# Attention stage of a hybrid trunk: small VectorE operations move to ScalarE, GpSimd and DMAs, and the scan reads its ones from PSUM

## The chip, the cores and the metric

The kernel runs on one core of a Trainium2 chip. The metric is the device time of one execution in microseconds (us). A core has a tensor engine for matmuls (TensorE, PE in the profile; PEld is its loading of weights), a vector engine (VectorE, DVE), a scalar engine (ScalarE, ACT), a general engine (GpSimd, POOL), and a queue engine that issues transfers here (SyncE, SP). Each engine takes its instructions in the order in which they stand in its own queue, and waits on semaphores for the others.

## What is computed

One layer on 1024 tokens of width 1024, all float32: a projection gives queries, keys and values for 8 heads of 64 and a convolution branch; both branches go through one output projection that is added to x, and a gated feed-forward block follows. The change lies in the attention:

```
z    = (q_t . k_s) / sqrt(64)                     # q, k normalised per head
beta = sigmoid(z);   log_one_minus = log_sigmoid(-z), masked to s < t
tail = reverse cumulative sum of log_one_minus over s, without the element itself
o_t  = sum over s < t of  beta[t,s] * exp(tail[t,s]) * v_s
x    = x + concat([attention, conv]) @ w_out
```

The kernel computes exp(tail) as a running product: the sigmoid of -z is taken, and a scan multiplies along the row from its end to its start.

## The kernel before

The stages follow one another: projections and convolution (about the first 257 us), attention with the convolution's half of the output projection between its groups (to about 508 us), the attention's half of the output projection with the second norm, the up projection, and the down projection.

Attention goes head by head (h = 0 to 7), and in a head through four groups g of 256 queries; a group is two blocks u of 128 queries, so that block tb = 2g + u has w = (tb + 1) * 128 keys to look at: scans of 128, 256 ... 1024 columns in a head. Work on a group is spread over three steps: `scores` of group i + 2, `weights` of group i + 1 and `values` of group i are written interleaved, by the positions in `at_value`, `at_score` and `at_weight`; `prep(i + 3)` prepares keys, queries and values of what comes. What stands in an engine's queue is then set by a scheduler that goes over the written program with a timing model of its own, so that a change in one place can move rows in others.

- `scores` (L471): PE makes z in a PSUM tile from the high and low parts of q (L490, L493, mask L492); ACT writes sigmoid(-z) into one of four row buffers `nb` (L494) and sigmoid(z) into `wt` (L495).
- `weights` (L499): DVE scans `nb` in place, multiplying by a column of ones `one` that is read w times (L505); then `wt` is multiplied by `nb` (L506), on DVE where w is 1024 and on GpSimd in the seven other blocks.
- `values` (L508): PE turns `wt` into a PSUM bank `wT` (L527), the rounded copy `th` is made (L533: on DVE in group 0, on ACT in groups 1 to 3), DVE makes the rest `tl` = wT - th (L537), PE adds the products with v to `po` (L543, L544). `finish` moves `po` to `attn_out` (ACT L554, DVE L555).
- `prep_k`, `prep_v`, `prep_q`: GpSimd splits keys and values (L418, L419) and writes each query twice side by side (L445); PE turns them (L430, L449); the turned keys go from PSUM to SBUF in two halves, one on DVE and one on ACT (both L433); ACT and DVE split the queries (L451, L452).
- `out_proj_conv(t)`, one token tile per head, is the list `between`: SP loads x (L400), PE multiplies (L158 to L160), DVE adds the product to x (L404, two halves), SP stores the sum (L406). The split of the activations `m` is L154 on ACT and L155 on DVE.

PSUM has eight banks: three in pool "s" (for `kT`, `qT`, `wT`), two in "o" (for `po` and the projection), two in "z", and one, `psx`, lent to a pool by `bank`: with `shared = "s"` every fourth bank of kind "s" comes from it, so that "s" has four in attention. After attention, `load_wo` fetches the other four row blocks of w_out (`rawo`) and splits them into `hio` (L154) and `loo` (L155), `out_proj_attn(t)` multiplies, adds x2 on DVE (L714) and stores; in the queues before, parts of this stand between rows of head 7.

Of the kernel before, what the change touches and what calls it, by code (L numbers as in the profile page):

```python
# [8 lines left out]
F32 = mybir.dt.float32  # L9
# [7 lines left out]
P = 128  # L17
S = 1024
# [20 lines left out]
def kernel(  # L39
# [32 lines left out]
    def f32(ap):  # L72
        return ap.bitcast(F32)
# [25 lines left out]
    def const(shape, dt, name):  # L99
        return cst.tile(shape, dt, tag=name, name=name)  # L100
# [244 lines left out]
        for _ in project(part, blk):  # L345
            pass
    in_ctx.close()
    shared = "s"
    turns["s"] = 0
    psz_ctx.close()  # L350
    psz = psz_ctx.enter_context(tc.tile_pool(name="ps_z", bufs=2, space=PSUM, reuse_waits="tile"))

    one = const([P, 1], F32, "one")
    nc.vector.memset(one, 1.0)


# [38 lines left out]
    def out_proj_conv(t):  # L395
        tile_of = {}

        def load():
            tile_of["x"] = ap_.tile([P, D], F32, tag="xt", name=f"xt{t}", bufs=2)
            nc.sync.dma_start(tile_of["x"], x_t[t])  # L400

        def add(n, cols, ps):
            xt = tile_of["x"]
            nc.vector.tensor_tensor(xt[:, cols], ps, xt[:, cols], op=ALU.add)  # L404
            if n == 1:
                nc.sync.dma_start(x_part[t], xt)  # L406

        first, *rest = out_proj(ap_, 1, t, conv_out, w_conv, add)
        return [lambda: (load(), first())] + rest
# [12 lines left out]
    def prep_k(h):  # L422

        blk, c0 = h // 4, (h % 4) * DH
        kst = part_of(keys, 1 + h % 2, S)
        khl = token_split(qkv["k", blk][:, :, c0:c0 + DH], part_of(keys, 0, S))
        for half in range(2):
            pt = bank("s", [P, 512], f"kT{h}_{half}", F32R)
            for i in range(4):
                nc.tensor.transpose(pt[:, i * P:(i + 1) * P],  # L430
                                    khl[:, 4 * half + i, :, :].rearrange("p a d -> p (a d)"), ident_r)
            copy = nc.scalar.copy if half else nc.vector.tensor_copy
            copy(kst[:, half * 512:(half + 1) * 512], f32(pt))  # L433
        return kst

    def prep_v(h):
        blk, c0 = h // 4, (h % 4) * DH
        return token_split(qkv["v", blk][:, :, c0:c0 + DH], part_of(rest, h % 2, S), e=h % 2)

    def prep_q(h, half):  # L440
        blk, c0 = h // 4, (h % 4) * DH
        spare = attn_out[:, 3, :] if h < 4 else qkv["q", 0].rearrange("p t c -> p (t c)")
        qd = part_of(spare, half, 512).rearrange("p (t a d) -> p t a d", a=2, d=DH)
        src = qkv["q", blk][:, 4 * half:4 * half + 4, c0:c0 + DH]
        nc.gpsimd.tensor_scalar(qd, src.unsqueeze(2).to_broadcast([P, 4, 2, DH]), 1.0, 0.0,  # L445
                                op0=ALU.mult, op1=ALU.add)
# [52 lines left out]
    def weights(i, u):  # L499
        w = (2 * (i % NG) + u + 1) * P  # L500
        o = S - w
        wt, nb = wts[i, u], nbq[i, u]
        rev = nb[:, S - 1:o - 1:-1] if o else nb[:, S - 1::-1]
        eng = nc.vector if w == S else nc.gpsimd
        return [lambda: nc.vector.tensor_tensor_scan(rev, rev, one.to_broadcast([P, w]), 1.0, op0=ALU.mult, op1=ALU.bypass),  # L505
                lambda: eng.tensor_tensor(wt[:, :w], wt[:, :w], nb[:, o + 1:S + 1], op=ALU.mult)]  # L506

    def values(i, sp):  # L508

# [19 lines left out]
        def high():  # L529
            nonlocal n_th  # L530
            n_th += 1
            d["th"] = part_of(rest, 6 + n_th % 2, 512).rearrange("p (j t) -> p j t", j=2)
            (nc.scalar.copy if g else nc.vector.tensor_copy)(d["th"], d["pt"])  # L533

        def low():
            d["tl"] = ap_.tile([P, 2, 256], F32R, tag="tl", name=f"tl{h}_{g}_{sp}")
# [26 lines left out]
    at_value = {"t": (0.07, 1.05, 4, 5.53), "h": (1.42, 3, 4.7, 7), "l": (2.87, 3.2, 5.2, 7.1), "p": (3.3, 6.33, 7.2, 7.3)}  # L563
    at_score = ((3.43, 2.27), (4.32, 2.05))
    at_weight = ((-0.19, 3.76), (3.43, 6.55))
    prep(0)
    for i in range(n_nb):
        nbs.append(ap_.tile([P, S + 1], F32, tag=f"nb{i}", name=f"nb{i}", bufs=1))
        nc.vector.memset(nbs[i][:, S:S + 1], 1.0)
    for i in range(-2, n_groups):  # L570
# [13 lines left out]
            finish(i)  # L584
        if i + 3 < n_groups:
            prep(i + 3)
        while between and n_between - len(between) < (i + 3) * n_between // (n_groups + 2) + FILL:
            between.pop(0)()
    at_ctx.close()
# [340 lines left out]
```

## Time and profile before

| | |
|---|---|
| Runs shown | median 1206.94 us of 3 (1205.44 to 1211.38) |
| The profiled execution | 1207.02 us, of which the profile's span is 1205.2 us; 16496 instructions |
| Busy in the span | PE 95%, PEld 80%, DVE 80%, ACT 53%, POOL 50% |
| TensorE clock granted, mean | 0.98 |
| DMA | 103.95 MB, mean 86 GB/s |

A row of instructions in the profile names the line, the engine and the operation, what is written from what (buffer numbers left out), the shape and the count; then the time that it kept the engine busy and the mean of one in ns; then how long the engine was idle just before, and what ended that. A row by stretches gives the busy time of PE, PEld, DVE, ACT and POOL in each stretch with their counts, then the granted clock, the DMA share and GB/s. A row by source line gives shortest, median and longest duration in ns. In a row of the timeline the first number is the start, the second the duration, and `x2` two instructions told together.

### The profile page before, as it was taken

To read this page: it belongs to the slowest core of one execution; us is meant where nothing else is said; L and a number is where in the kernel's file an instruction comes from. 1 tells how busy PE (TensorE), PEld (TensorE's weight loads), DVE (VectorE), ACT (ScalarE), POOL (GpSimd) and SP (SyncE) were. 2 spreads that over 40 slices of the span, in tenths; PEclk is the share of its full clock that TensorE was granted. 3 is DMA by queue.
4 is the path that set the end of the run, shared out by engine and by line. 5 is a ranking of instruction groups with operands and counts; after the bars stand their busy time and mean duration, and the time that the engine had idled before them with its cause. 6 is when DMAs were issued, how large, how long until landed. Compare 5 with 4: busy or idle time off the path is not lost.

```text
span 1205.2 us, 16496 instructions
## 1 busy us (share of the span) xinstructions
PE 1141.8 (95%) x5926; PEld 958.6 (80%) x5926; DVE 958.9 (80%) x1167; ACT 633.8 (53%) x1371; POOL 608.6 (50%) x466
## 2 busy tenths in 40 slices
PE   7999999988888888997999999999999999999998
PEld 5888999977777777775888888888888877888887
DVE  6399998468988889789887777777777579978887
ACT  6346667655665567366444333333434356666762
POOL 4068973455755554168643322332233157778873
PEclk9999999998998899998999999999999999999999
DMA  7121111011011013353232222323222261333133
GB/s 246 39 70 53 35 36 36 19 56 68 36 36 36 36 35 107 126 188 105 71 105 70 88 88 71 97 65 101 70 88 83 92 230 67 140 140 114 41 126 140
DMA packets 82080, 103.95 MB, mean 86 GB/s; under 512 B 3438, under 2 KB 63054, under 8 KB 81998
## 3 DMA queue, kind: packets, MB, share of 16 engines
q1 hardware_dynamic: 81710, 101.84, 25.1%
q8 instruction: 47, 0.77, 0.3%
q10 hardware_dynamic: 288, 1.05, 0.2%
q14 instruction: 35, 0.29, 0.1%
HBM read 78.76 MB, written 24.12 MB: 85 GB/s over the span
## 4 chain that ended last, share of the span: by engine, by line
PE 74%; DVE 12%; POOL 5%; issue 4%; ACT 3%; DMA 1%; SPq 0%; POOLq 0%; DVEq 0%; ACTq 0%
PE dn L890 16%; PE u_S L160 6%; PE u_S L159 6%; PE u_S L158 6%; PE u L160 5%; PE u L159 5%; PE u L158 5%; DVE nb L505 4%; DVE tl L537 2%; PE po L544 1%; PE wT L527 1%; POOL conv_out L283 1%; DVE conv L277 1%; PE op L160 1%; PE op L158 1%
## 5 line engine op out<-in xcount | busy, mean ns | idle before, releaser
L890 PE MATMUL dn<-wd,wd 128*128 128x512 f32 x924 | 213.8, 392 | 5.1 <-DVE c L893 2.6
L890 PEld LDWEIGHTS dn<-wd,wd 128*128 128x128 f32 x924 | 172.6, 188 | 46.0 <-DVE c L893 4.6
L893 DVE TENSOR_TENSOR c<-dn,c 128x512 f32<-128x512 f32 x144 | 95.2, 683 | 25.2 <-PE dn L890 23.9
L506 POOL TENSOR_TENSOR wt<-wt,nb 128x128 f32<-128x128 f32 (+6 forms) x56 | 80.2, 1444 | 68.3 <-DVE nb L505 56.2
L277 DVE SCALAR_TENSOR_TENSOR conv<-cpad,cols_b,conv 128x1024 f32<-128x1024 f32 x84 | 108.2, 1288 | 2.4
L283 POOL TENSOR_TENSOR conv_out<-conv_out,attn_out 128x1024 f32<-128x1024 f32 x32 | 81.3, 2540 | 53.0 <-ACT attn_out L282 51.0
L801 ACT CAST wd<-rawd 128x512 fp32r<-128x512 f32 x154 | 85.4, 618 | 39.8 <-DMA rawd<-act_d 24.0
L505 DVE TENSOR_TENSOR_SCAN nb<-nb,one 128x128 f32<-128x128 f32 (+3 forms) x64 | 97.3, 1544 | 4.7 <-ACT nb L494 4.6
L154 ACT CAST aS<-rawu 128x512 fp32r<-128x512 f32 x66 | 40.7, 620 | 99.8 <-PE u_S L160 58.9
L699 POOL TENSOR_TENSOR s<-rawu 128x512 f32<-128x512 f32 x21 | 30.2, 1440 | 124.1 <-DMA rawu<-in_w_up_dram 123.5
L800 ACT COPY whole<-rawd 128x512 f32<-128x512 f32 x110 | 63.4, 585 | 40.3 <-DVE wd L802 18.8
L802 DVE TENSOR_TENSOR wd<-whole,wd 128x512 fp32r<-128x512 f32 x110 | 73.5, 683 | 8.3 <-ACT whole L800 7.2
L802 POOL TENSOR_TENSOR wd<-rawd,wd 128x512 fp32r<-128x512 f32 x44 | 57.4, 1327 | 35.5 <-ACT wd L801 34.8
L154 ACT CAST a<-rawu 128x512 fp32r<-128x512 f32 x66 | 40.8, 621 | 56.6 <-PE u_S L160 37.7
L544 PE MATMUL po<-tl,rest 128*128 128x256 f32 x160 | 50.7, 336 | 19.1 <-DVE tl L537 19.0
L527 PE MATMUL wT<-ident,wt 128*128 128x128 f32 x288 | 50.8, 295 | 17.4 <-POOL wt L506 15.7
L494 ACT ACTIVATE nb<-z 128x512 f32<-128x512 f32 (+3 forms) x96 | 48.0, 501 | 35.6 <-PE z L493 31.6
L757 DVE SCALAR_TENSOR_TENSOR y<-gv,cols_a,y 128x1023 f32<-128x1023 f32 (+1 forms) x44 | 57.8, 1314 | 10.3 <-ACT y L755 10.3
L155 DVE TENSOR_TENSOR aS<-rawu,aS 128x512 fp32r<-128x512 f32 x66 | 63.1, 959 | 3.2 <-ACT aS L154 2.8
L155 DVE TENSOR_TENSOR a<-rawu,a 128x512 fp32r<-128x512 f32 x65 | 48.9, 753 | 16.4 <-ACT a L154 16.4
L705 POOL TENSOR_TENSOR rawu<-rawu 128x512 f32<-128x512 f32 x22 | 31.0, 1411 | 58.1 <-DVE a L155 56.2
L533 ACT CAST rest<-wT 128x512 fp32r<-128x512 f32 x72 | 41.7, 596 | 34.6 <-PE po L543 29.0
(266 smaller groups left out, 3658.4 us busy)
## 6 DMA issues: line engine op xcount, KB each, us to landing
rawu<-in_w_up_dram SPq DMA_DIRECT2D x44, 512.0 KB, 3.8
act_d<-y SPq DMA_DIRECT2D x22, 512.0 KB, 2.6
rawd<-act_d SPq DMA_DIRECT2D x22, 512.0 KB, 6.6
rawd<-in_w_down_dram SPq DMA_DIRECT2D x22, 512.0 KB, 5.9
rawo<-in_w_out_dram SPq DMA_DIRECT2D x8, 512.0 KB, 3.8
xt<-in_x_dram SPq DMA_DIRECT2D x8, 512.0 KB
x_part<-xt SPq DMA_DIRECT2D x8, 512.0 KB, 2.7
x<-x_part SPq DMA_DIRECT2D x8, 512.0 KB, 3.5
```

The source lines that it names most:

```text
L154: nc.scalar.copy(hi, src)
L155: lo_engine.tensor_tensor(lo, src, f32(hi), op=ALU.subtract)
L158: nc.tensor.matmul(ps, a_hi, b_hi, start=first, stop=False)
L159: nc.tensor.matmul(ps, a_hi, b_lo, start=False, stop=False)
L160: nc.tensor.matmul(ps, a_lo, b_hi, start=False, stop=last)
L277: nc.vector.scalar_tensor_tensor(own, src, tap(c, j), own, op0=ALU.mult, op1=ALU.add)
L283: nc.gpsimd.tensor_tensor(acc, acc, term, op=ALU.add)
L505: return [lambda: nc.vector.tensor_tensor_scan(rev, rev, one.to_broadcast([P, w]), 1.0, op0=ALU.mult, op1=ALU.bypass), lambda: eng.tensor_ ...
L801: nc.scalar.copy(t[:, 0], src)
L802: lo_engine.tensor_tensor(t[:, 1], whole, f32(t[:, 0]), op=ALU.subtract)
L890: nc.tensor.matmul(ps, a[:, tok], b, start=first and m == 0, stop=last and m == 2, skip_group_check=True)
L893: nc.vector.tensor_tensor(sums[c][s], ps, sums[c][s], op=ALU.add)
```

## The change

Six edits, all in the attention stage. (1) `one` is a column of a PSUM bank, taken from `psx`; that bank is lent to nobody any more (`shared = ""`), so pool "s" has three banks. (2) The product of the output projection is copied from PSUM to a tile `prod` on ACT and added to x on GpSimd, in place of one addition on DVE. (3) Both halves of the turned keys are copied on ACT. (4) The multiplication of `wt` for w = 1024 is on GpSimd like the others. (5) `th` is made on ACT in group 0 as well. (6) The doubled queries are written by two DMAs of SP each, in `load_q`, two steps ahead of `prep_q`, and not by GpSimd.

```diff
-    shared = "s"
-    turns["s"] = 0
+    shared = ""
...
-    one = const([P, 1], F32, "one")
+    one = psx.tile([P, 512], F32, tag="bank", name="one")[:, :1]
     nc.vector.memset(one, 1.0)
...
         def add(n, cols, ps):
-            xt = tile_of["x"]
-            nc.vector.tensor_tensor(xt[:, cols], ps, xt[:, cols], op=ALU.add)
+            xt, prod = tile_of["x"], ap_.tile([P, 512], F32, tag="prod", name=f"prod{t}_{n}", bufs=1)
+            nc.scalar.copy(prod, ps)
+            nc.gpsimd.tensor_tensor(xt[:, cols], prod, xt[:, cols], op=ALU.add)
...
-            copy = nc.scalar.copy if half else nc.vector.tensor_copy
-            copy(kst[:, half * 512:(half + 1) * 512], f32(pt))
+            nc.scalar.copy(kst[:, half * 512:(half + 1) * 512], f32(pt))
...
-    def prep_q(h, half):
+    qds = {}
+    def load_q(h, half):
         blk, c0 = h // 4, (h % 4) * DH
         spare = attn_out[:, 3, :] if h < 4 else qkv["q", 0].rearrange("p t c -> p (t c)")
         qd = part_of(spare, half, 512).rearrange("p (t a d) -> p t a d", a=2, d=DH)
         src = qkv["q", blk][:, 4 * half:4 * half + 4, c0:c0 + DH]
-        nc.gpsimd.tensor_scalar(qd, src.unsqueeze(2).to_broadcast([P, 4, 2, DH]), 1.0, 0.0,
-                                op0=ALU.mult, op1=ALU.add)
+        for a in range(2):
+            nc.sync.dma_start(qd[:, :, a, :], src)
+        qds[h, half] = qd
+    def prep_q(h, half):
+        qd = qds.pop((h, half))
...
-        eng = nc.vector if w == S else nc.gpsimd
         return [lambda: nc.vector.tensor_tensor_scan(rev, rev, one.to_broadcast([P, w]), 1.0, op0=ALU.mult, op1=ALU.bypass),
-                lambda: eng.tensor_tensor(wt[:, :w], wt[:, :w], nb[:, o + 1:S + 1], op=ALU.mult)]
+                lambda: nc.gpsimd.tensor_tensor(wt[:, :w], wt[:, :w], nb[:, o + 1:S + 1], op=ALU.mult)]
...
-            (nc.scalar.copy if g else nc.vector.tensor_copy)(d["th"], d["pt"])
+            nc.scalar.copy(d["th"], d["pt"])
...
+        if 4 <= i + 5 < n_groups and (i + 5) % 2 == 0:
+            load_q((i + 5) // NG, (i + 5) % NG // 2)
```

Lines move by up to ten: the scan is L511 and the multiplication L512 after, `tl` L543, the addition to x L405, the store L407.

VectorE's queue in head 5 before, from the scan of 896 columns to that of 512 (a scan is printed under the name SCALAR_TENSOR_TENSOR; the first digit behind `wt`, `tl`, `xt` is the head or token tile, the last number a buffer's):

```order
L505 SCALAR_TENSOR_TENSOR nb2_2809<-nb2_2809,one_2772 128x896
L505 SCALAR_TENSOR_TENSOR nb3_2811<-nb3_2811,one_2772 128x1024
L537 TENSOR_TENSOR tl5_2_0_4442<-wT5_2_0_4431,rest_2778 128x512
L537 TENSOR_TENSOR tl5_2_1_4445<-wT5_2_1_4436,rest_2778 128x512
L506 TENSOR_TENSOR wt5_7_4343<-wt5_7_4343,nb3_2811 128x1024
L505 SCALAR_TENSOR_TENSOR nb0_2805<-nb0_2805,one_2772 128x128
L505 SCALAR_TENSOR_TENSOR nb1_2807<-nb1_2807,one_2772 128x256
L404 TENSOR_TENSOR xt5_4330<-op5_1_4482,xt5_4330 128x512
L155 TENSOR_TENSOR m6_4616<-conv_out_148,m6_4616 128x512
L505 SCALAR_TENSOR_TENSOR nb2_2809<-nb2_2809,one_2772 128x384
L537 TENSOR_TENSOR tl5_2_2_4471<-wT5_2_2_4459,rest_2778 128x512
L505 SCALAR_TENSOR_TENSOR nb3_2811<-nb3_2811,one_2772 128x512
```

The same piece after:

```order
L511 SCALAR_TENSOR_TENSOR nb2_2812<-nb2_2812,one_2772 128x896
L511 SCALAR_TENSOR_TENSOR nb3_2814<-nb3_2814,one_2772 128x1024
L511 SCALAR_TENSOR_TENSOR nb0_2808<-nb0_2808,one_2772 128x128
L543 TENSOR_TENSOR tl5_2_0_4479<-wT5_2_0_4468,rest_2778 128x512
L543 TENSOR_TENSOR tl5_2_1_4482<-wT5_2_1_4473,rest_2778 128x512
L511 SCALAR_TENSOR_TENSOR nb1_2810<-nb1_2810,one_2772 128x256
L511 SCALAR_TENSOR_TENSOR nb2_2812<-nb2_2812,one_2772 128x384
L155 TENSOR_TENSOR m6_4656<-conv_out_148,m6_4656 128x512
L543 TENSOR_TENSOR tl5_2_2_4508<-wT5_2_2_4496,rest_2778 128x512
L511 SCALAR_TENSOR_TENSOR nb3_2814<-nb3_2814,one_2772 128x512
```

The multiplication `wt` and the addition `xt` are gone from the queue; the rest stands in nearly the same order.

TensorE's queue at the end of head 7 before, where the output projection of token tile 0 (`op0`, with the split weights `hio`, `loo`) stands ahead of the last turned weights `wT7_3`:

```order
L544 MATMUL po7_2_4972<-tl7_2_1_4987,rest_2778 128x256
L158 MATMUL op0_0_5152<-hio0_5123,m0_5149 128x512
L159 MATMUL op0_0_5152<-loo0_5124,m0_5149 128x512
L158 MATMUL op0_1_5166<-hio0_5123,m0_5149 128x512
L159 MATMUL op0_1_5166<-loo0_5124,m0_5149 128x512
```

The end of attention there after:

```order
L549 MATMUL po7_2_5018<-rest_2778 128x256
L550 MATMUL po7_2_5018<-tl7_3_2_5091,rest_2778 128x256
L549 MATMUL po7_2_5018<-rest_2778 128x256
L550 MATMUL po7_2_5018<-tl7_3_3_5103,rest_2778 128x256
L549 MATMUL po7_2_5018<-rest_2778 128x256
L550 MATMUL po7_2_5018<-tl7_3_3_5103,rest_2778 128x256
L158 MATMUL op0_0_5200<-hio0_5171,m0_5197 128x512
```

The 48 matmuls of `op0` and `op1`, which stood between rows of head 7, now follow its last product; the splits into `hio` and `loo` stand behind it too, on ACT and DVE.

The queue of SP at the same place before (transfers only):

```order
L406 DMA x_part6_78<-xt6_4614 128x1024
L368 DMA rawo0_5125<-in_w_out_dram 128x1024
L368 DMA rawo1_5131<-in_w_out_dram 128x1024
L368 DMA rawo2_5137<-in_w_out_dram 128x1024
L368 DMA rawo3_5143<-in_w_out_dram 128x1024
L626 DMA x2_0_5147<-x_part0_72 128x1024
```

And after:

```order
L407 DMA x_part6_78<-xt6_4654 128x1024
L367 DMA rawo0_5173<-in_w_out_dram 128x1024
L367 DMA rawo1_5179<-in_w_out_dram 128x1024
L367 DMA rawo2_5185<-in_w_out_dram 128x1024
L407 DMA x_part7_79<-xt7_4942 128x1024
L690 DMA rawu0_0_5569<-in_w_up_dram 128x8x128
L690 DMA rawu0_2816_5571<-in_w_up_dram 128x8x128
L367 DMA rawo3_5191<-in_w_out_dram 128x1024
L636 DMA x2_0_5195<-x_part0_72 128x1024
```

The last of the four weight loads and the loads of x2 now stand behind the store of the last x tile, `x_part7_79`, which waits for GpSimd's last addition.

More of the change, by code (lines that the diff above doesn't have):

```diff
@@ L565 @@
     at_weight = ((-0.19, 3.76), (3.43, 6.55))
+    for half in range(2):
+        load_q(0, half)
     prep(0)
```

## The prediction

> **What bounds the kernel now.** I read the page's totals first, then the busy time by stretches, then the groups of the attention stage by engine and shape, the waits there, and last one head's timeline.
>
> ```profile
> span 1205.2 us, 16496 instructions
> PE 1141.8 (95%) x5926; PEld 958.6 (80%) x5926; DVE 958.9 (80%) x1167; ACT 633.8 (53%) x1371; POOL 608.6 (50%) x466
> 20.00:257.00 237.00, 234.55 (x1617) 218.46 (x1616) 183.91 (x174) 137.24 (x484) 129.26 (x94) 1.00 0.14 42
> 259.00:495.00 236.00, 197.59 (x1178) 165.33 (x1179) 210.14 (x226) 148.84 (x314) 131.25 (x95) 0.91 0.17 58
> 600.00:960.00 360.00, 360.00 (x1575) 295.35 (x1574) 267.99 (x322) 132.21 (x188) 111.05 (x76) 1.00 0.27 87
> 420.50:442.50 22.00, 17.30 (x105) 14.19 (x105) 20.16 (x21) 14.09 (x30) 14.67 (x10) 0.97 0.14 48
> 442.50:449.30 6.80, 6.80 (x51) 6.48 (x51) 5.32 (x8) 4.10 (x10) 2.56 (x3) 0.85 0.00 1
> ```
>
> Before and after attention TensorE is busy all the time (234.55 of 237, 360 of 360 us). In attention it is not: 197.6 of 236 us, at a mean clock of 0.91, while VectorE is busy for 210.1. All six edits lie there. Inside one head (the last two rows) VectorE is full for 22 us (20.16) and waits a little in the remaining 6.8, where TensorE is full. So the stage is VectorE's, head by head, with a short stretch of waiting for each other at the head's end.
>
> ```profile
> 302.13 1.48 DVE L505 TENSOR_TENSOR_SCAN nb<-nb,one 128x640 f32<-128x640 f32 x1
> 426.80 0.69 DVE L555 TENSOR_TENSOR attn_out<-po,attn_out 64x512 f32<-64x512 f32 x1 [0.93 <-ACT attn_out L554]
> 432.60 1.29 DVE L537 TENSOR_TENSOR tl<-wT,rest 128x512 fp32r<-128x512 f32 x2
> 433.81 1.41 DVE L506 TENSOR_TENSOR wt<-wt,nb 128x1024 f32<-128x1024 f32 x1
> 435.14 0.99 DVE L505 TENSOR_TENSOR_SCAN nb<-nb,one 128x128 f32<-128x128 f32 x2
> 436.06 0.66 DVE L404 TENSOR_TENSOR xt<-op,xt 128x512 f32<-128x512 f32 x1
> 436.64 0.84 DVE L155 TENSOR_TENSOR m<-conv_out,m 128x512 fp32r<-128x512 f32 x1
> 438.28 0.66 DVE L537 TENSOR_TENSOR tl<-wT,rest 128x512 fp32r<-128x512 f32 x1
> 476.72 1.47 DVE L505 TENSOR_TENSOR_SCAN nb<-nb,one 128x640 f32<-128x640 f32 x1
> PEld po L544 <- DVE tl L537: 22.6, 17, 2.7
> ```
>
> From the scan of 640 columns in head 1 to that in head 7 six heads pass in 174.6 us, 29.1 each. TensorE's largest waits for VectorE are those for `tl`.
>
> **The scan and GpSimd.** Besides its own work VectorE loses time to GpSimd, and GpSimd to it:
>
> ```profile
> L505 DVE TENSOR_TENSOR_SCAN nb<-nb,one 128x1024 f32<-128x1024 f32 x8 | 21.6, 2706 | 0.0
> L505 DVE TENSOR_TENSOR_SCAN nb<-nb,one 128x896 f32<-128x896 f32 x8 | 19.9, 2485 | 3.6 <-ACT nb L494 3.6
> L505 DVE TENSOR_TENSOR_SCAN nb<-nb,one 128x768 f32<-128x768 f32 x8 | 15.3, 1919 | 1.0 <-ACT nb L494 1.0
> L505 DVE TENSOR_TENSOR_SCAN nb<-nb,one 128x640 f32<-128x640 f32 x8 | 12.1, 1518 | 0.1
> L505 DVE TENSOR_TENSOR_SCAN nb<-nb,one 128x512 f32<-128x512 f32 x8 | 12.9, 1611 | 0.0
> L505 DVE TENSOR_TENSOR_SCAN nb<-nb,one 128x384 f32<-128x384 f32 x8 | 8.1, 1017 | 0.0
> L505 DVE TENSOR_TENSOR_SCAN nb<-nb,one 128x128 f32<-128x128 f32 x8 | 3.3, 407 | 0.0
> L506 DVE TENSOR_TENSOR wt<-wt,nb x8: 1192/1483/2147, 287.1 to 495.1; 128x1024 f32<-128x1024 f32 x8
> L537 DVE TENSOR_TENSOR tl<-wT,rest x80: 657/680/693, 269.4 to 507.0; 128x512 fp32r<-128x512 f32 x80
> L418 POOL TENSOR_SCALAR keys<-k x8: 620/1870/1973, 244.3 to 420.6; 128x512 fp32r<-128x512 f32 x8
> ```
>
> The mean of 512 columns (1611) is above that of 640 (1518), so length alone does not set it. Through 128 and 640 columns runs 2.17 ns a column; by that line 384, 512, 768, 896 and 1024 columns should take 962, 1240, 1796, 2073 and 2351 ns. They take 55, 371, 123, 412 and 355 more, eight times each: 10.5 us in the stage, 1.31 a head. `wt` on VectorE, which also has two inputs in SBUF, ranges from 1192 to 2147 ns; `tl`, with one of its two in PSUM, stays within 657 to 693 over 80 instructions beside the same GpSimd. GpSimd's copy of the keys, for which 620 ns is enough, takes 1870 in the median. So I take it that two SBUF inputs make VectorE and GpSimd exclude each other, and that a scan with its ones in PSUM is free of it, as `tl` is.
>
> [...]
>
> **The change, edit by edit,** with these rows for what is moved:
>
> ```profile
> L506 DVE TENSOR_TENSOR wt<-wt,nb 128x1024 f32<-128x1024 f32 x8 | 12.7, 1590 | 0.0
> L404 DVE TENSOR_TENSOR xt<-op,xt 128x512 f32<-128x512 f32 x16 | 10.7, 671 | 0.0
> L433 DVE CAST keys<-kT 128x512 fp32r<-128x512 f32 x8 | 5.5, 688 | 9.0 <-PE kT L430 9.0
> L533 DVE CAST rest<-wT 128x512 fp32r<-128x512 f32 x8 | 5.5, 686 | 2.3 <-PE po L543 2.3
> L533 ACT CAST rest<-wT 128x512 fp32r<-128x512 f32 x70 | 40.6, 597 | 30.6 <-PE po L543 25.0 <-PE wT L527 3.2 <-DVE tl L537 2.3
> L506 POOL TENSOR_TENSOR wt<-wt,nb 128x512 f32<-128x512 f32 x8 | 9.7, 1215 | 8.7 <-DVE nb L505 7.5 <-ACT keys L451 1.2
> L506 POOL TENSOR_TENSOR wt<-wt,nb 128x768 f32<-128x768 f32 x8 | 13.4, 1671 | 0.0
> rawu<-in_w_up_dram SPq DMA_DIRECT2D x44, 512.0 KB, 3.8
> SPq L406 <- DVE xt L404: 178.1, 8, 27.1
> L277 DVE SCALAR_TENSOR_TENSOR conv<-cpad,cols_b,conv 128x1024 f32<-128x1024 f32 x84 | 108.2, 1288 | 2.4
> ```
>
> VectorE loses 12.7 + 10.7 + 5.5 + 5.5 = 34.4 us of work, and 10.5 of exclusion: 45 of its 210. That is not the saving; it is taken place by place.
>
> *`wt` of 1024 columns to GpSimd.* In the full stretch VectorE gets 1.33 us a head back (433.81 to 435.14). GpSimd's rows of 512 and 768 columns give 1.78 ns a column, so 1024 take about 2.1 us: `wt` is ready 2.1 us after its scan, where it was 2.5 (432.60 to 435.14), because it no longer stands behind two `tl`. No loss for the turning of it.
>
> *The addition to x.* Two per head. One stands in the full stretch (0.58 from start to start), the other in front of a wait of 0.93 us for `attn_out`, which would only grow; I count 0.58. ACT gets 16 copies at about 0.60 (by its `th` row) = 9.6 us, GpSimd 16 additions at 1.2 = 19. Nobody waits for x but the store, and behind the store in SP's queue.
>
> *Keys and group 0's `th` to ACT.* They stand in the head's last stretch, in chains; 0.69 on VectorE becomes 0.60 to 0.63 on ACT, 16 times: 9.8 us on ACT, nothing gained or lost. ACT has 148.8 of 236 us busy; with 19.4 more it is at 168. Its queue is in order, so in the worst case the two copies of the product push two sigmoids a head back by 0.6 each: 0 to 1.2 us a head; I take 0, since ACT sat idle 30.6 us before `th` alone, and keep 1.2 for the range.
>
> *Doubled queries by DMA.* 32 transfers of 128 KB more on SP, 16 operations fewer on GpSimd. No row shows such small pieces; the nearest is 3.8 us for 512 KB, and the loads stand two of four steps, about 14 us, ahead. SP waits 178 us in all for the addition before its stores, and the query loads now stand behind those stores: each can be late by as much as GpSimd's addition is late against the order. Price 0, and up to a few us where one is caught.
>
> *The ones in PSUM.* `tl`, with the same kinds of input, takes as long as what has both in SBUF would without a collision, so 0. VectorE's longest comparable case sets the other end: 1288 ns for the convolution's step with PSUM in and out (L277, 1024 columns), against the shortest `wt`, 1192: 0.1 us a scan, 0.8 a head. A gain is excluded: 2.17 ns a column is about twice what `tl` needs, so reading is not what limits it.
>
> *The bank.* Pool "s" has three banks for 14 fillings a head (ten `wT`, two `kT`, two `qT`). Before, the third `tl` of group 2 came at 438.28, 5.7 us after the first two, holding a bank all that time. In the new queue it still comes after the scan of 384. I take 0, because the new order places the turning of `wt` behind the `tl` that free a bank; the other end is a rival.
>
> *The end of attention.* The 48 matmuls of `op0` and `op1` no longer fill TensorE's gaps in head 7 but follow it, and the fourth weight load stands behind the last store of x. Before, the second addition of `op1` came 29.7 us after head 7's scan of 640 columns:
>
> ```profile
> 506.37 0.68 DVE L714 TENSOR_TENSOR x<-op,x 128x512 f32<-128x512 f32 x1
> ```
>
> In the new order I get about 4.7 us to the scan of 896, 4.4 for it and that of 1024, 2.1 for `wt`, 4 for turning, `th`, `tl` and the last products, 2 for the first split, and 11 for the 48 matmuls: 28. Equal, then; the head's own shortening does not come on top. From −3 to +6.
>
> *Sum.* In the full stretch a head saves 1.33 + 0.58 + 1.31 = 3.22 us, so 29.1 becomes 25.9. Seven heads run up to the scan that the last paragraph starts from: 7 × 3.22 = 22.5, and the end is equal. The profiled execution took 1207.02 us (span 1205.2 and 1.8 around it), within 0.1 of the median, 1206.94. 1207.0 − 22.5 = **1184.5 us**. The most that the stage can give is until TensorE is full: 236 − 197.6 = 38, so 1169.
>
> **Rivals.** *All of it, and the clock.* The granted clock is 0.91 in attention and 1.00 in the full stages. If TensorE no longer pauses, its own 197.6 us shrink, and both chains and matmuls get shorter: saving 30 to 40, about 1172. Against it: the head's last stretch keeps its waits. *ACT and the chains give half back.* The 1.2 us for ACT's copies and 0.6 for the scan's PSUM read leave 1.4 a head: 10 us, 1197. For it: ACT is between every two engines here. *Nothing moves.* The scan collides as before, or TensorE's own chain at 17.3 of 22 us is as long: 1201 to 1213. Against it: 20.16 of 22. *Slower: three banks.* With a bank short, each of the four turnings of group 3 waits for a `tl` that stands behind scans. It eats the 3.2 us if each waits 0.8, and makes the kernel slower by 0.5% (6 us, 0.9 a head) from 1.0 each: about 1217 at 1.2 each. For it: `tl` is what TensorE waits for already (22.6 us). Against it: `tl` stands in a shorter queue.
>
> *GpSimd as the chain.* A `wt` of 1024 columns takes 2.1 us there against 1.33 in VectorE's queue. If TensorE then waits for the last `wt` of a head, 0.8 of the 3.22 us go back: 2.4 a head, 1190, inside the forecast's own range and given no chance apart. For it: TensorE's waits for `wT` before. Against it: GpSimd loses its own collisions, and has 105 of 236 us free.
>
> [...]
>
> **How the numbers follow.** The sum as forecast (1175 to 1193) 0.48; more, with the clock, 0.14; half given back (1193 to 1201) 0.17; nothing 0.09; slower 0.12. Faster by over 0.5%, about what a measurement of this kernel can tell from no change, is the first three: 0.79. The range 1167 to 1203 leaves out the slower case and a little on both sides.
>
> **What would show it.** Scans on one line of 2.2 ns a column with no spread; GpSimd's key copy at 0.62 us throughout; a head of about 26 us from scan to scan; VectorE near 165 of a stage of about 213; ACT near 168. The prediction is wrong if scans stay spread, if TensorE's waits for `wT` (a bank) or `qT` (a load) take the place of those for `tl`, or if the end of attention grows by more than 6 us.

## The result, and the profile after

The changed kernel takes 1216.14 us (median of 14 runs, 1211.03 to 1217.84) against 1207.83 us (14 runs): the ratio is 1.0055, 95% interval 1.0038 to 1.0073. It is worked out apart from the medians, so it need not be their quotient. The kernel became slower, by about 8 us; the forecast was 23 us faster. The profiled execution has this span and these totals:

```profile
span 1215.9 us, 16551 instructions
PE 1153.8 (95%) x5926; PEld 960.4 (79%) x5926; DVE 927.9 (76%) x1127; ACT 651.6 (54%) x1403; POOL 598.8 (49%) x474
```

By stretches (busy time of PE, PEld, DVE, ACT, POOL with counts; granted clock, DMA share, GB/s), the attention and the up projection after:

```profile
259.00:495.00 236.00, 200.88 (x1224) 166.62 (x1224) 176.35 (x194) 169.45 (x353) 123.69 (x106) 0.93 0.23 72
600.00:960.00 360.00, 360.00 (x1545) 289.62 (x1544) 274.41 (x319) 130.82 (x186) 110.69 (x74) 1.00 0.26 85
```

VectorE's load in the attention fell from 210 to 176 us (near 165 was expected), and ScalarE's rose to 169. The second row was not expected: TensorE is full in both kernels, at clock 1.00, but got 1545 matmuls done in 360 us where it was 1575. Nothing of the change lies there.

The scans, and GpSimd's instructions beside them, after (mean ns of one, then VectorE's or GpSimd's idle time before it):

```profile
L511 DVE TENSOR_TENSOR_SCAN nb<-nb,one 128x1024 f32<-128x1024 f32 x8 | 18.1, 2264 | 0.0
L511 DVE TENSOR_TENSOR_SCAN nb<-nb,one 128x896 f32<-128x896 f32 x8 | 16.2, 2020 | 9.6 <-ACT nb L501 9.5
L511 DVE TENSOR_TENSOR_SCAN nb<-nb,one 128x640 f32<-128x640 f32 x8 | 11.9, 1485 | 18.9 <-ACT nb L501 18.9
L511 DVE TENSOR_TENSOR_SCAN nb<-nb,one 128x512 f32<-128x512 f32 x8 | 9.6, 1202 | 0.0
L511 DVE TENSOR_TENSOR_SCAN nb<-nb,one 128x128 f32<-128x128 f32 x8 | 3.2, 396 | 0.0
L512 POOL TENSOR_TENSOR wt<-wt,nb 128x1024 f32<-128x1024 f32 x8 | 16.0, 2003 | 5.6 <-DVE nb L511 5.2 <-ACT nb L501 0.4
L419 POOL TENSOR_SCALAR keys<-k 128x512 fp32r<-128x512 f32 x7 | 4.3, 621 | 8.9 <-PE kT L431 8.9
```

They lie on one line of 2.08 ns a column, and the key copy is back at 621 ns. But the scan of 640 columns, which waited for nothing before (0.1 us), now finds VectorE idle for 18.9 us, waiting for ScalarE's sigmoids. The waits of the attention after say what ScalarE waits for:

```profile
POOL xt L405 <- ACT prod L404: 30.6, 9, 7.5
ACT prod L404 <- PE op L160: 29.9, 15, 2.9
DVE nb L511 <- ACT nb L501: 28.5, 13, 2.9
```

The copy `prod` stands in ScalarE's queue ahead of sigmoids whose z is there, and waits there for the product. TensorE has a wait that it did not have before: for a PSUM bank, to put the turned weights `wT` in, until VectorE has split a query out of it.

```profile
PE wT L533 <- DVE rest L459: 6.4, 6, 1.3
```

The prediction named such a wait as a sign of being wrong.

At the end of the attention, the scan of 640 of head 7, the splits of w_out, the second addition of `op1` and the last addition of the stage, after:

```profile
473.13 3.13 DVE L511 TENSOR_TENSOR_SCAN nb<-nb,one 128x640 f32<-128x640 f32 x2 [2.44 <-ACT nb L501]
490.92 2.94 ACT L154 CAST hio<-rawo 128x1024 fp32r<-128x1024 f32 x3
497.64 1.05 ACT L154 CAST hio<-rawo 128x1024 fp32r<-128x1024 f32 x1 [3.78 <-DMA rawo<-in_w_out_dram]
508.56 0.69 DVE L724 TENSOR_TENSOR x<-op,x 128x512 f32<-128x512 f32 x1 [1.47 <-PE op L160]
551.74 0.47 PE L158 MATMUL u<-b11h,a 128*128 128x512 f32 x1
```

And before:

```profile
471.50 1.05 ACT L154 CAST hio<-rawo 128x1024 fp32r<-128x1024 f32 x1
477.76 2.98 ACT L154 CAST hio<-rawo 128x1024 fp32r<-128x1024 f32 x3
549.86 0.48 PE L158 MATMUL u<-b11h,a 128*128 128x512 f32 x1
```

The four splits ran beside head 7 before and come behind it after, the last one waiting for its load.

Such rows cut every profiled execution into four pieces that add up to its span: up to the scan of 640 in head 1; the six heads from there to the same scan in head 7 (mean of one); from that scan to the first product of the up projection; from there to the end. All in us; the medians stand beside those of the kernel before that ran with them, and the ratios with their 95% intervals. The kernel before had medians of 1207.4 to 1209.3 beside the different kernels, so a difference between two rows with different kernels before is uncertain by some 2 us. The time up to head 1 of one execution scatters too: before, e2 and e5 have the same order of instructions on every engine, but for the memset of a column, and took 302.1, 301.1 and 303.3.

| kernel | median (before) | ratio | to head 1 | a head | end of attention | up and down |
|---|---|---|---|---|---|---|
| before | 1207.83 | | 302.1 | 29.10 | 73.1 | 655.3 |
| after | 1216.14 (1207.83) | 1.0055, 1.0038–1.0073 | 301.8 | 28.56 | 78.6 | 664.2 |
| e1_after_pad | 1206.54 (1208.2) | 0.9979, 0.9958–1.0 | 298.9 | 28.33 | 78.5 | 655.7 |
| e2_before_pad | 1215.09 (1208.2) | 1.0052, 1.0029–1.0075 | 301.1 | 29.04 | 73.2 | 663.8 |
| e3_only_ones | 1195.86 (1208.2) | 0.9893, 0.9841–0.9945 | 298.0 | 27.35 | 76.1 | 655.6 |
| e4_after_no_add | 1194.66 (1208.2) | 0.9867, 0.9818–0.9917 | 301.0 | 27.66 | 71.1 | 655.6 |
| e5_both_pad | 1202.66 (1209.31) | 0.994, 0.991–0.9971 | 303.3 | 29.13 | 74.1 | 650.8 |
| e6_only_wt | 1210.71 (1209.31) | 0.9997, 0.9963–1.0031 | 300.2 | 30.13 | 73.6 | 656.0 |
| e7_ones_wt | 1192.46 (1209.31) | 0.9864, 0.9798–0.9931 | 298.8 | 26.88 | 75.9 | 655.7 |
| e8_only_add | 1224.68 (1209.31) | 1.0125, 1.0051–1.0199 | 303.0 | 29.66 | 83.0 | 655.7 |
| e9_before_grow | 1216.2 (1207.42) | 1.008, 1.0053–1.0107 | 302.2 | 28.92 | 83.0 | 655.7 |
| e10_prod_in_tl | 1196.55 (1207.42) | 0.9892, 0.9862–0.9922 | 300.6 | 27.72 | 71.7 | 655.9 |
| e11_only_bank | 1217.44 (1207.42) | 1.0085, 1.0047–1.0122 | 303.2 | 30.51 | 73.7 | 655.8 |
| e12_1345_equal_places | 1191.51 (1207.42) | 0.9851, 0.9818–0.9884 | 298.3 | 28.02 | 71.3 | 650.1 |
| e13_14_equal_places | 1185.1 (1207.68) | 0.982, 0.9802–0.9838 | 297.1 | 26.64 | 75.9 | 650.2 |
| e14_six_both_mended | 1191.3 (1207.68) | 0.9861, 0.9845–0.9878 | 300.6 | 28.18 | 73.0 | 650.2 |
| e15_no_act_copies | 1200.05 (1207.68) | 0.9936, 0.9917–0.9956 | 303.2 | 27.05 | 74.3 | 656.0 |
| e16_146_equal_places | 1189.82 (1207.68) | 0.985, 0.9832–0.9867 | 300.0 | 26.66 | 76.3 | 650.6 |

From before to after: −0.3, −3.3 in six heads (six times 3.22, 19.3, was forecast), +5.5 at the end of attention (0 was forecast), +8.9 behind it (0 was forecast).

### The profile page after: what moved, and what is told of

It is laid out like the page before. It is cut to its first block, busy times and chain, and to the rows that moved or that the text cites. A ratio compares the mean times of both kernels' runs of the same rounds, so it can differ in the third digit from the quotient of the medians.

```text
span 1215.9 us, 16551 instructions
## 1 busy us (share of the span) xinstructions
PE 1153.8 (95%) x5926; PEld 960.4 (79%) x5926; DVE 927.9 (76%) x1127; ACT 651.6 (54%) x1403; POOL 598.8 (49%) x474
## 4 chain that ended last, share of the span: by engine, by line
PE 79%; DVE 8%; ACT 6%; POOL 3%; issue 3%; DMA 2%; SPq 0%; ACTq 0%; POOLq 0%; DVEq 0%
PE dn L900 16%; PE u_S L158 7%; PE u_S L160 7%; PE u_S L159 7%; PE u L158 5%; PE u L160 5%; PE u L159 5%; PE op L160 2%; PE wT L533 2%; PE op L158 2%; PE op L159 2%; DVE nb L511 2%; POOL conv_out L283 1%; PE q L158 1%; PE q L160 1%
## 5 line engine op out<-in xcount | busy, mean ns | idle before, releaser
L511 DVE TENSOR_TENSOR_SCAN nb<-nb,one 128x128 f32<-128x128 f32 (+3 forms) x64 | 83.2, 1338 | 28.5 <-ACT nb L501 28.5
L512 POOL TENSOR_TENSOR wt<-wt,nb 128x128 f32<-128x128 f32 (+3 forms) x64 | 79.1, 1245 | 50.9 <-DVE nb L511 32.4
L812 DVE TENSOR_TENSOR wd<-whole,wd 128x512 fp32r<-128x512 f32 x110 | 73.2, 682 | 1.4 <-ACT whole L810 1.1
L155 DVE TENSOR_TENSOR aS<-rawu,aS 128x512 fp32r<-128x512 f32 x66 | 69.2, 1052 | 2.8 <-ACT aS L154 2.4
L767 DVE SCALAR_TENSOR_TENSOR y<-gv,cols_a,y 128x1023 f32<-128x1023 f32 (+1 forms) x44 | 61.2, 1392 | 13.0 <-ACT y L765 13.0
L715 POOL TENSOR_TENSOR rawu<-rawu 128x512 f32<-128x512 f32 x22 | 34.1, 1552 | 60.4 <-DVE a L155 58.5
L543 DVE TENSOR_TENSOR tl<-wT,rest 128x512 fp32r<-128x512 f32 x80 | 53.3, 681 | 13.1 <-ACT rest L539 12.3
L539 ACT CAST rest<-wT 128x512 fp32r<-128x512 f32 x80 | 47.1, 594 | 21.5 <-DVE tl L543 7.9
L550 PE MATMUL po<-tl,rest 128*128 128x256 f32 x160 | 45.8, 309 | 10.1 <-DVE tl L543 9.8
```

Of the source, the lines that this page charges most:

```text
L155: lo_engine.tensor_tensor(lo, src, f32(hi), op=ALU.subtract)
L812: lo_engine.tensor_tensor(t[:, 1], whole, f32(t[:, 0]), op=ALU.subtract)
```

## The experiments

### Where the up projection's 8 us come from

In the built program every engine's instructions of the up projection stand in the same order before and after, with the same PSUM banks. What differs is addresses. `one` took a 32-byte place beside the other constants in SBUF; with `one` in PSUM, every tile allocated behind them on that side lies 32 bytes lower. The stationary operand `a` of the up products starts at 32 within 128 bytes before and at 0 after; the moving operand `b`, allocated from the other side, stays at 96. Three kernels change only that; the order of the instructions is otherwise the one they start from.

```diff
 # e1_after_pad: the changed kernel
+    pad = const([P, 1], F32, "pad"); nc.vector.memset(pad, 1.0)
     one = psx.tile([P, 512], F32, tag="bank", name="one")[:, :1]
 # e2_before_pad: the kernel before
+    pad = const([P, 1], F32, "pad"); nc.vector.memset(pad, 1.0)
     one = const([P, 1], F32, "one")
 # e5_both_pad: e2, and between the pools `wu` and `ffn`, whose tiles are b
+    padp = up_ctx.enter_context(tc.tile_pool(name="padp", bufs=1, side="right", ...))
+    nc.vector.memset(padp.tile([P, 1], F32, tag="pad2", name="pad2"), 1.0)
```

> The changed kernel with one unused column of 4 bytes beside the other constants in SBUF, so that every tile that lies behind the constants has the byte address that it had before the change (the change had taken the column `one` out of there and moved them 32 bytes down). The order of the instructions on every engine is that of the changed kernel, but for the one memset of the column. Theory (address): the 1848 products of the dense up stage, one every 0.234 us after and 0.230 before, go back to 0.230, the stage from 440.8 to 432.8 us, and the time from 1216.1 to about 1208.0. Rival (the up stage is slower for another reason: what the attention left behind, transfers, heat): 1216, and the stage still at 440.

> The kernel before with one more unused column of 4 bytes beside the constants: the same tiles lie 32 bytes higher than before, and nothing else changes. Theory (address, the place within 64 bytes decides): the up stage goes to 440 us, the time to about 1216. Theory (address, only a place that is a multiple of 128 bytes is slow): no change, 1208, since the tiles then start at 64 within 128. Rival (addresses do nothing): 1208.

> As the run with the kernel before moved up by 32 bytes (`a` at 64 within 128, 1215.1 us), and the other operand of the up products, `b`, moved down by 32 bytes too, from 96 to 64 within 128. Theory (what counts is whether the stationary `a` and the moving `b` start at the same place within 64 bytes): the up stage is back at 432.8 us and the time at 1207.8. Rival (the place of `a` alone counts): the stage stays at 440.8, the time at 1215.

The same stretch of the up projection in e1:

```profile
600.00:960.00 360.00, 360.00 (x1574) 295.50 (x1573) 264.42 (x319) 132.83 (x190) 110.30 (x75) 1.00 0.26 85
```

in e2:

```profile
600.00:960.00 360.00, 360.00 (x1545) 289.28 (x1544) 274.19 (x317) 131.29 (x186) 107.78 (x73) 1.00 0.26 84
```

and in e5:

```profile
600.00:960.00 360.00, 360.00 (x1590) 298.10 (x1589) 268.53 (x326) 133.64 (x191) 111.15 (x76) 1.00 0.27 88
```

360 us over the counts gives the time of one matmul:

| starts of a and b within 128 bytes | kernels | us of one matmul |
|---|---|---|
| 64 and 64 | e5 | 0.2264 |
| 32 and 96 | before, e1 | 0.2286, 0.2287 |
| 0 and 96 | after | 0.2330 |
| 64 and 96 | e2 | 0.2330 |

An unused column of 4 bytes gives the changed kernel 9.6 us back: 8.0 in the up projection, which takes 432.8 us again from its first product to the first of the down projection, where it was 440.8; the rest is mostly the time up to head 1, which scatters by as much between kernels that are alike there. Moving the kernel before by 32 bytes costs it 7 us, without any other change. In these runs a matmul took 0.2330 us where the two starts differ by 32 or 96 within 128 bytes, 0.2286 and 0.2287 where they differ by 64, and 0.2264 where they are equal. The stage's time agrees in every kernel: 432.8 in all that have 32 and 96, and 428.8 to 429.0 in the four further kernels below that have 64 and 64. Equal starts at other places than 64 were not tried. For e5 the theory had the stage at 432.8 us; it took 428.8, less than in any kernel before it. The place of `a` alone does not decide: e2 and e5 have it at the same 64 and differ in the start of `b` alone (96 and 64), and in the pace, 0.2330 against 0.2264 us. So the place of one operand against the other counted here; why it does was not tried.

### Where the end of attention's time comes from

`prod` is 2 KB a partition in the attention's pool, which grows downwards: `nb0` begins at 104288 instead of 106336. `loo3`, the last split of w_out, lies at 102048 to 106144 before and 32 bytes lower after. It now overlaps `nb0` and must wait until the attention's last scans have done with it, and with it the 48 products of `op0` and `op1`: all 48 of them stood ahead of the attention's last product before, none after (the expectations below speak of 34 and 32; the queues of the kernel before and of e10 have all 48 there). e9 takes the 2 KB without the edit, e10 makes the edit without the 2 KB, e8 makes the edit alone.

```diff
 # e8_only_add: the kernel before with the second edit of the change, nothing else
 # e9_before_grow: the kernel before
             if n == 1:
+                t == 0 and nc.vector.memset(ap_.tile([P, 512], F32, tag="grow", name="grow", bufs=1)[:, :1], 1.0)
 # e10_prod_in_tl: e1
-    ap_.tile([P, 512], F32, tag="prod", name=f"prod{t}_{n}", bufs=1)
+    ap_.tile([P, 512], F32, tag="tl", name=f"prod{t}_{n}")
```

> The kernel before with the second edit alone: the add of the out-projection as a copy on ScalarE and an add on GpSimd. The prediction's step: 7 x 0.58 = 4 us faster, 1204. Theory now (the copy waits in ScalarE's queue ahead of the sigmoids, and op0 and op1 fall behind the end of attention): slower by about the 12 us that undoing it gave, 1220.

> The kernel before with one unused tile of 2 KB a partition in the attention's pool, as large as `prod`: the four `nb` tiles then begin at 104288 instead of 106336, and nb0 covers the end of loo3 (102048 to 106144), the last split of w_out's attention half. No copy and no add is moved. Theory (place: loo3, and with it the products of op0 and op1, must wait until the attention has done with nb0): 0 of those 48 products stand ahead of the last product of the attention instead of 34, and the time is that of the run with the second edit alone less what its copies cost in the heads (0.6 us each): about 1208 + 10 = 1218. Rival (the copy on ScalarE and the add on GpSimd cost it): 1208.

> The changed kernel with the addresses of `a` kept, and `prod` taken from the two buffers of `tl`, which have its size: the attention's pool is as small as before, nb0 no longer covers loo3, and 32 products of op0 and op1 stand ahead of the attention's last. Copy and add stay on ScalarE and GpSimd. Theory (place): the end of the attention gets its 7.4 us back, 1206.5 - 7.4 = 1199; what then lies between 1199 and the 1194.7 of the run without the second edit is the wait of ScalarE for the product. Rival (the copy and the add cost it all): 1206.

The first splits of w_out on ScalarE and the first additions of the next stage, from the timeline of e9:

```profile
498.58 1.99 ACT L154 CAST hio<-rawo 128x1024 fp32r<-128x1024 f32 x2
508.65 1.29 DVE L714 TENSOR_TENSOR x<-op,x 128x512 f32<-128x512 f32 x2 [0.82 <-PE op L160]
```

and a split early and the last one, with the first addition, from that of e10:

```profile
462.95 1.08 ACT L154 CAST hio<-rawo 128x1024 fp32r<-128x1024 f32 x1
471.03 1.05 ACT L154 CAST hio<-rawo 128x1024 fp32r<-128x1024 f32 x1
483.30 0.69 DVE L724 TENSOR_TENSOR x<-op,x 128x512 f32<-128x512 f32 x1 [2.15 <-PE op L160]
```

An unused tile costs the kernel before 8.8 us, all of it at the end of attention (73.1 to 83.0). The changed kernel with `prod` in the buffers of `tl` gains 10.0 us over e1, 6.8 of them at that place and 3.7 in the heads, whose order changed with it. The 2 KB, not the copy, made the end late: all 48 products stand ahead of the attention's last in e10, none in e9. e8, at +15.4, holds the same 9.9 us there and 0.6 a head, for which its profile has a row:

```profile
ACT prod L403 <- PE op L160: 9.5, 7, 2.2
```

> The changed kernel with the addresses kept and the second edit undone: the add of the out-projection is on VectorE again. Theory (the copy `prod` stands in ScalarE's queue ahead of the sigmoids and waits there for the product): VectorE no longer waits 2.7 us ahead of the scan of 640, heads some 2 us shorter less the 0.58 that VectorE takes back, 1208 - 7 x 1.4 = about 1198. Rival (the copy costs nothing, ScalarE is late for other reasons): 1208 + 7 x 0.58 = 1212.

```diff
 # e4_after_no_add: e1 with the second edit undone
-            nc.scalar.copy(prod, ps)
-            nc.gpsimd.tensor_tensor(xt[:, cols], prod, xt[:, cols], op=ALU.add)
+            nc.vector.tensor_tensor(xt[:, cols], ps, xt[:, cols], op=ALU.add)
```

e4 is 11.9 us faster than e1, about what the theory had, but for another reason in the main: 0.67 us a head, 4.0 in six, comes from the heads, and 7.4 from the end, which the 2 KB made. Against e10, which keeps the edit and drops the 2 KB, e4 gains 1.9 us, less than the two intervals can tell apart. In e10's order ScalarE's wait of 30 us for `prod` behind the product is gone, and its heads are 0.61 us shorter than e1's. So that wait, long as it is in the profile, goes with about 0.6 us a head.

### The bank, the ones and the multiplication

```diff
 # e11_only_bank: the kernel before
-    shared = "s"
+    shared = ""
     one = const([P, 1], F32, "one")
+    held = psx.tile([P, 512], F32, tag="bank", name="held")[:, :1]      # written, never read
 # e3_only_ones: the first edit, and the pad of e1
 # e6_only_wt: the fourth edit
-        eng = nc.vector if w == S else nc.gpsimd      # and eng.tensor_tensor -> nc.gpsimd.tensor_tensor
 # e7_ones_wt: e3 and e6 together
```

> The kernel before with three banks for the transposes instead of four, and nothing else: the ones stay in SBUF, the fourth bank is held by a tile that nothing reads. The prediction's step (the bank costs nothing): 1208. Rival (three banks make TensorE wait): the 1217 of the prediction's rival.

> The kernel before with the first edit alone: the ones in a PSUM bank, three banks for the transposes instead of four; the addresses in SBUF are kept. Theory (the bank costs at least what the shorter scans bring): 1208 to 1214, TensorE waiting for a bank of qT or wT, scans at 2.08 ns a column. Rival (the bank is free, as predicted): 7 heads x 1.31 = 9.2 us faster, 1198.6.

> The kernel before with the fourth edit alone: the mult of the weights of width 1024 on GpSimd, the ones still in SBUF. The prediction's step: 7 x 1.33 = 9.3 us faster, 1198.5. Rival (GpSimd, which still gives way to the scans, hands the weights over late, and another engine waits in place of VectorE): 1207 or more.

> The first and the fourth edit, addresses kept. The prediction's step, if VectorE bounds the head: 1195.9 - 9.3 = 1186.6. Rival (with the ones in PSUM the head is no longer bounded by VectorE: TensorE is busy for 86% of it and waits for `tl`, so what VectorE gives away comes back as its waits): 1193 to 1197.

Scans of 1024 and 512 columns and GpSimd's `wt` (56 instructions) in e11:

```profile
L505 DVE TENSOR_TENSOR_SCAN nb<-nb,one 128x1024 f32<-128x1024 f32 x8 | 22.8, 2853 | 0.0
L505 DVE TENSOR_TENSOR_SCAN nb<-nb,one 128x512 f32<-128x512 f32 x8 | 12.7, 1586 | 0.0
L506 POOL TENSOR_TENSOR wt<-wt,nb 128x128 f32<-128x128 f32 (+6 forms) x56 | 77.2, 1384 | 87.7 <-DVE nb L505 59.7 <-ACT hio L154 10.1 <-ACT nb L494 7.4
```

and in e3:

```profile
L505 DVE TENSOR_TENSOR_SCAN nb<-nb,one 128x1024 f32<-128x1024 f32 x8 | 18.1, 2267 | 0.0
L505 DVE TENSOR_TENSOR_SCAN nb<-nb,one 128x512 f32<-128x512 f32 x8 | 9.6, 1202 | 0.0
L506 POOL TENSOR_TENSOR wt<-wt,nb 128x128 f32<-128x128 f32 (+6 forms) x56 | 64.0, 1142 | 99.8 <-DVE nb L505 57.8 <-ACT rest L533 18.8 <-ACT hio L154 8.7
```

Three banks cost 10.0 us by the medians, 5.7 to 14.7 by the interval. With fewer banks the scheduler also writes another order, so this is the price of both. Waits over heads 1 to 6, 298 to 462 us, before:

```profile
PE po L544 <- DVE tl L537: 14.6, 10, 2.5
DVE nb L505 <- ACT nb L494: 3.0, 3, 1.4
```

and in e11:

```profile
PE po L544 <- DVE tl L537: 14.9, 9, 2.5
DVE nb L505 <- ACT nb L494: 8.6, 17, 0.7
```

No row of e11 has TensorE waiting for a bank of `wT`, and its wait for `tl` is what it was; VectorE waits longer for the sigmoids. So the price is shown, and the slower rival's way to it, turnings that wait for a `tl`, is not. That e11's 1217.4 meets that rival's 1217 is luck: the rival priced the bank at four times 1.2 us a head, 33.6 us in seven heads, set off by all the other savings.

e11 and e3 have the same order on every engine and differ in where the ones lie: that is worth 21.6 us, 3.16 us a head, and e3 came out faster than both of its expectations. All 64 scans together take 15.0 us less (100.9 and 85.9); the scan of 1024 columns alone gets 586 ns shorter, and GpSimd's `wt` 242 ns each, 1.7 us a head. So the first edit is worth −12.3 us as a whole.

e6 shows no gain, as its rival had it: with the ones in SBUF GpSimd's longer list brings nothing. On top of e3 the multiplication brings 3.4 us, between the two expectations and inside the intervals. Waits of e7 over heads 1 to 6, 298 to 462 us:

```profile
PE po L544 <- DVE tl L537: 12.1, 12, 1.9
DVE nb L505 <- ACT nb L494: 7.4, 15, 0.6
```

TensorE waits for `tl` nearly as long as before the change (14.6 us in the same stretch), and VectorE waits for ScalarE, as it does in e11 and e3 (8.6 and 6.9 us). That no one engine holds the head any more, so that time taken off VectorE comes back as a wait, fits these rows; it was not tried by itself.

### All six without the two placements, and the best version

```diff
 # e14_six_both_mended: e10, with a and b both at 64 within 128 (a second pad, and e5's padp)
 # e15_no_act_copies: e10 with the third and fifth edit undone
 # e12_1345_equal_places: edits 1, 3, 4 and 5, a and b at 64
 # e13_14_equal_places: edits 1 and 4, a and b at 64
 # e16_146_equal_places: e13 and the sixth edit
```

> All six edits, with `prod` in the buffers of `tl` and with `a` and `b` both at 64 within 128: nothing is left out of the change but its two effects on placement. Theory (the costs add): 1196.6 - 4 = 1192.6, 23 us under the changed kernel. Rival (they overlap): 1196.

> The changed kernel with the old addresses of `a` and `prod` in the buffers of `tl` (1196.6), and the third and fifth edit undone: the first key half and th of group 0 are copied on VectorE again, 3 copies of 0.65 us a head. Theory (ScalarE, which is busy for 73% of the head and in whose queue the sigmoids wait, is the late one; its copies take back part of the gain): 1190 to 1194. Rival (they cost nothing, as predicted; VectorE's time is what bounds): 1197 or more.

> Edits one, three, four and five (ones in a bank, both key copies and the copy of every th on ScalarE, the mult of width 1024 on GpSimd), without the add and without the copies of q by transfers, and `a` and `b` both at 64 within 128. Theory (places): 4 us less than at the old places, so with ScalarE's copies at nothing, as predicted, 1192.5 - 4 = 1188.5; at 0.3 us lost for each head 1190.6. Rival (they free VectorE for what bounds it): 1184.

> The first and the fourth edit, with `a` and `b` both at 64 within 128. Theory (places): the 1192.5 of these edits at the old places less 4 us, 1188.5, the fastest so far. Rival (the stage that the places shorten waits for its loads instead): 1191 or more.

> The first, fourth and sixth edit at equal places: beside the run without the sixth it gives the price of doubling q by transfers. The prediction's step: 0, the same time as that run, about 1188.5. Rival (GpSimd's 1.24 us a head are worth something, since VectorE waited for its q copy 1.7 us in six heads): 1186. Rival (16,000 packets under 512 bytes more hold up other loads): 1191.

With its two placements mended the whole change takes 1191.3 us, 16 us under before and 25 under the kernel as changed; the costs add (1192.6 was expected). e13, with two of the six, takes 1185.1 us, ratio 0.982 (0.9802 to 0.9838): the fastest version here, faster than both kernels. It came out below the 1188.5 expected, in part since "up and down" gains more than the up projection's 4 us: e14 and e13 have 650.2 where their partners at the old places, e10 and e7, have 655.9 and 655.7. The doubled queries by transfers cost 4.7 us on top of e13 by the medians, but the intervals, 0.9832 to 0.9867 and 0.9802 to 0.9838, just overlap, and the heads take the same time (26.66 and 26.64): 2.9 us of the difference lie in the time up to head 1, which scatters. ScalarE's copies cost 6.4 us on top of e13 (e12), whereas in e10 taking them out costs 3.5 (e15); both pairs of intervals overlap, so the sign of their price in the whole is not settled. In the heads both pairs point one way: with the copies on ScalarE a head is 1.38 us longer (e12 against e13) and 0.67 (e10 against e15). Waits from 298 to 455 us, most of heads 1 to 6, in e12:

```profile
PE wT L527 <- DVE rest L452: 6.7, 6, 1.3
DVE nb L505 <- ACT nb L494: 14.4, 12, 2.5
```

and in e13:

```profile
DVE nb L505 <- ACT nb L494: 7.5, 15, 0.6
```

In e12 VectorE waits twice as long for the sigmoids behind ScalarE's copies, and TensorE for `wT` until VectorE has released a query's bank, which e13 has no row for. The changed kernel has that wait too, 6.4 us; e3 and e7, which also have three banks but not the copies, do not.

## Why the prediction was wrong, point by point

| step | forecast, us | measured, us | from |
|---|---|---|---|
| three banks | 0 | +10.0 (5.7 to 14.7) | e11 against before |
| ones in PSUM | −9.2 | −21.6 | e3 against e11 |
| `wt` of 1024 on GpSimd | −9.3 | −3.4, not resolved | e7 against e3 |
| doubled queries by DMA | 0 | +4.7, not resolved; none of it in the heads | e16 against e13 |
| key and `th` copies on ScalarE | 0 | −3.5, or +6.4 in another order; neither resolved | e10 against e15; e12 against e13 |
| the addition itself | −4.1 | +1.9, not resolved | e10 against e4 |
| the 2 KB of `prod` | 0 | +10.0, of which 6.8 at the end (+8.8 in the kernel before) | e1 against e10 (e9 against before) |
| the address of `a` | none | +9.6 | after against e1 |
| sum | −22.6 | +7.7 | after against before: +8.3 |

The last row closes only with −3.5 for the copies; with +6.4 the sum is 17.6. The rows come from kernels with different orders, so that it closes is in part luck.

- **VectorE's saving is the head's saving: failed.** Of 19.3 us forecast for six heads, 3.3 came. VectorE got lighter, but waits 28.5 us for ScalarE's sigmoids where it waited 4.6, and TensorE for a bank. By the heads in the table: 27.35 with the first edit, 26.88 with the fourth added (e7), 27.66 with the third, fifth and sixth added (e4), 28.33 with the second (e1). The sixth adds nothing in the heads (e16), so ScalarE's copies gave back 0.8 us a head for the third and fifth edit and 0.7 for the second, which with `prod` in the buffers of `tl` (e10, 27.72) is 0.1. "I take 0" for ScalarE was the wrong end of the prediction's own 0 to 1.2; of its rivals, "ACT and the chains give half back" had this part of the mechanism. How much of it each wait costs stays open.
- **Exclusion of scan and GpSimd: right, as far as the rows go.** The scans are on one line (2.08 ns a column), the key copy is at 621 ns where its median was 1870, and the scan of 128 columns takes 396 ns where it took 407, so the read from PSUM shows no cost. e11 and e3 show that the place of the ones does it; that the two engines exclude each other over two SBUF inputs stays the author's reading of the rows. The size was off by more than two: the forecast counted VectorE's excess of 10.5 us alone, while the scans got 15.0 us shorter from e11 to e3, and GpSimd's instructions shorter too. That the latter makes up the rest of the 21.6 is argued, not shown.
- **"The bank: I take 0": failed.** It costs 10.0 us, through an order in which VectorE waits for sigmoids, as far as the rows show. The slower rival was right that the bank has a price, but had it at 33.6 us and by another wait; that the changed kernel's 1216.1 lies near its 1217 is luck.
- **"Equal, then" at the end of attention: failed.** 28 us were forecast from the scan of 640 to the second addition of `op1`; it took 35.4 (473.13 to 508.56). The order shown ahead of the prediction already had the 48 products behind the attention. The cause taken for it, the store of x in SP's queue, was not tried by itself; e9 and e10 show that the overlap of `nb0` and `loo3` is enough.
- **`wt` and the addition: prices right, gains not.** `wt` of 1024 took 2003 ns (2.1 us forecast). e7 brings a third of the 9.3 by the medians, e6 nothing. "Nobody waits for x but the store" overlooked that the copy itself waits, in ScalarE's queue.
- **DMAs and ScalarE's copies at nothing.** For the DMAs it is not refuted: 4.7 us in the whole, not resolved, and 0.02 us a head. For the copies it failed in the heads (0.67 and 1.38 us a head); in the whole their sign is open.
- **Missing altogether: what an allocation moves.** Of the three largest losses two, 9.6 and 10.0 us, are not work (the third is the bank). Without them the change is at 1191.3, in the forecast's own range of 1175 to 1193, though not by the forecast's sum: the ones bring more than was counted, and the bank and ScalarE's copies take it back.

## What to carry to other kernels

An edit that adds or removes a buffer changes the addresses of all that is allocated behind it. Compare the addresses of the built program before and after as one compares the order: a tile that newly covers another one can carry a wait (9.9 us at the end of attention in e9), and the starts of two matmul operands moved the pace of a full TensorE here by up to 3% (0.2264 to 0.2330 us a matmul). When a stage that the change does not touch gets slower, count its instructions in equal stretches of time first: one row for each kernel showed it here.

## What the runs showed of the hardware that was not expected

Beside the matmul's pace by the starts of its operands (0.2264, 0.2286 and 0.2330 us), heads of the same work come in two lengths in e13, and the granted clock goes with them: four of 25.88 to 25.91 us at 1.00, and one of 27.34 us at 0.94. Heads 4 and 5 of e13, and two-microsecond stretches of head 5:

```profile
374.84:400.75 25.91, 22.85 (x153) 19.40 (x152) 22.61 (x27) 17.81 (x40) 14.50 (x14) 1.00 0.13 42
400.75:428.09 27.34, 24.29 (x153) 20.86 (x152) 22.89 (x27) 17.83 (x40) 14.51 (x14) 0.94 0.12 39
414.75:416.75 2.00, 0.91 (x9) 0.71 (x7) 2.00 (x3) 1.41 (x3) 0.42 (x2) 1.00 0.65 262
416.75:418.75 2.00, 1.18 (x8) 0.98 (x8) 2.00 (x4) 0.58 (x1) 1.16 (x2) 1.00 0.26 21
418.75:420.75 2.00, 1.92 (x10) 1.86 (x11) 1.31 (x3) 0.58 (x1) 0.71 (x1) 0.61 0.62 242
420.75:422.75 2.00, 2.00 (x11) 2.00 (x11) 0.69 (x1) 1.27 (x2) 0.62 (x1) 0.54 0.04 8
```

Both heads have 153 matmuls and the same 2.0 us of waits for `tl`. Behind 4 us in which TensorE was busy for 2.1, the clock falls to 0.61 and 0.54 for 4 us, and the head is 1.43 us longer. What sets the fall off is not shown. 25.9 us is also the head that was forecast, and the four heads at clock 1.00 have it; that is luck, since e13 has two of the six edits. Of the changed kernel's six heads five have a clock of 0.88 to 0.94, so part of what they lack to the forecast may be the clock's; that was not tried apart.
